# Seven block products instead of eight in the up projections of two feed-forward networks, with weight pools by tile size

## The chip, the cores and the metric

The kernel runs on one core of one Trainium2 chip. Its engines are TensorE (PE in the profile: matmuls; PEld: the loads of its stationary side), VectorE (DVE), ScalarE (ACT), GpSimd (POOL) and SyncE (SP), which here only starts transfers. The metric is the device time of one execution in microseconds (us), lower is better.

## The reference

Two blocks of a network on 512 tokens of width 1024 in f32. The first block has a feed-forward network (ffn1), a mixer, a cross attention and a second feed-forward network (ffn2); the second has a mixer, a plain network and an embedding branch. Only the two feed-forward networks are changed:

```python
D_MODEL, SEQ, D_FF = 1024, 512, 2816

def swiglu(x, w1, w3, w2):
    return (jax.nn.silu(x @ w1) * (x @ w3)) @ w2
...
        f = swiglu(rms_norm(h, ffn1_pre_g[l]), ffn1_w1[l], ffn1_w3[l], ffn1_w2[l])
        h = h + 0.5 * rms_norm(f, ffn1_post_g[l])
...
        f = swiglu(rms_norm(h, ffn2_pre_g[l]), ffn2_w1[l], ffn2_w3[l], ffn2_w2[l])
        h = h + 0.5 * rms_norm(f, ffn2_post_g[l])
```

## The kernel before

Everything is kept with features on the 128 partitions and the 512 tokens along the row: the width 1024 is 8 tiles, the hidden width 2816 is 22. A product has f32 accuracy by splitting both sides into a high part, rounded to the matmul's format, and the residue (low part), and doing three matmuls into the same bank: high by high, high by low, low by high (`mm3`, L283 to L285). So one output tile of an up projection is 8 x 3 = 24 matmuls of 512 columns.

A weight tile is loaded by SP into a raw buffer (`wr`), cast to its high part by ScalarE (`wh`, L246), and VectorE subtracts to get the residue (`wl`, L247). The pools hold 2 raw tiles and 5 of each part, each sized for 8 blocks of 128 x 128. In names of the profile x tiles are the normalised inputs, b, u and t tiles are slots of 512 elements, h the running state, `mm` and `lg` the banks of results.

`ffn` goes over the hidden tiles in chunks (6, 8 and 8 in ffn1; 7, 7 and 8 in ffn2). For a chunk it runs w1 and w3 for each tile, takes the product of the two with the activation (factors of the norm on VectorE, L560 and L564; activation on ScalarE; product on GpSimd, L565; split by ScalarE, L356, and VectorE, L357), and then projects the chunk down: 8 output tiles, each summed over the chunk's tiles and added to the sum so far (L543). The first 4 or 5 products of a stage run by halves of 256 tokens while the norm still computes (`begin`, with weights split into b and u slots: lead tiles). The last 5 or 4 outputs of the last down projection run by halves too: all first halves (A), then the second ones (B), which fill the time in which the next norm needs only A ("late" in the tables; kept in `self.rest`, run in `begin` of the next stage).

Each engine takes its instructions in the order that the program's scheduler wrote, and every engine waits for the others by semaphores; the order within one engine is fixed once the program is built.

Of the kernel before, what the change touches and what calls it, by code (L numbers as in the profile page):

```python
# [19 lines left out]
P = 128  # L20
# [147 lines left out]
BANKS = {k: v for k, v in K["banks"].items() if v}  # L168
SLOTS = dict(zip("btu", K["slots"]))


# [4 lines left out]
class Net:  # L176
    def __init__(self, ctx, tc, a):
        self.tc, self.nc, self.a = tc, tc.nc, a
        pool = lambda name, bufs, **k: ctx.enter_context(tc.tile_pool(name=name, bufs=bufs, **k))
        self.cp = pool("cp", 1)  # L180
        self.xp = pool("xp", 16)
        self.slots = {t: pool(t + "p", n) for t, n in SLOTS.items()}
        self.sp = pool("sp", 2)
        self.wr = pool("wr", 2)
        self.wh = pool("wh", 5)
        self.wl = pool("wl", 5)

# [12 lines left out]

        self.lead = self.nc.vector
# [30 lines left out]
    def pa(self):  # L232
        return self.bank("tt")


    def load(self, src, shape):

        nc = self.nc
        n = int(np.prod(shape[1:]))
        raw, hi, lo = (  # L240
            pool.tile([P, n], dt, tag=tag, name=self.nm(tag), padded_shape=[P, 8 * P])
            for pool, dt, tag in ((self.wr, F32, "wr"), (self.wh, F32R, "wh"), (self.wl, F32R, "wl")))
# [16 lines left out]
    def lead_weights(self, w, n, nk, k0=0, tag="b"):  # L259

        nc = self.nc
        raw = self.wr.tile([P, nk, P], F32, tag="wr", name=self.nm("wr"), padded_shape=[P, 8, P])
        src = self.a[w][n, :, k0 : k0 + nk, :]
# [16 lines left out]

    def mm3(self, ps, a, b, first, last):
        mm = self.nc.tensor.matmul
        mm(ps, lhsT=a[0], rhs=b[0], start=first, stop=False)  # L283
        mm(ps, lhsT=a[0], rhs=b[1], start=False, stop=False)  # L284
        mm(ps, lhsT=a[1], rhs=b[0], start=False, stop=last)  # L285

# [51 lines left out]
    def stream(self, jobs, tail=0, spare=0):  # L338
# [8 lines left out]
        for (_, _, xs, _, put), wt in zip(jobs[mid:], wts):  # L347
            put(self.lin(wt, xs, A), A)
            self.rest.append(lambda xs=xs, put=put, wt=wt: put(self.lin(wt, xs, B), B))

    def split(self, src, parts, scale=None):
# [198 lines left out]
    def ffn(self, pre, post, w1, w3, w2):  # L550
# [5 lines left out]
        def up(n):  # L556
# [11 lines left out]
            return u, [(w1, n, xs, 0, first), (w3, n, xs, 0, second)]  # L568

        c = 0  # L570
        for size in K["sizes:" + self.phase]:
            us, jobs = [], []
            for n in range(c, c + size):
# [848 lines left out]
```

## Time and profile before

| | us |
|---|---|
| Time, median of 3 runs | 2154.33 (2153.68 to 2159.0) |
| The profiled execution: its own time | 2151.55 |
| its span, first to last instruction | 2149.4 |
| TensorE busy in the span | 2083.3 (97%) |
| VectorE busy | 1287.4 (60%) |
| ScalarE busy | 907.5 (42%) |
| GpSimd busy | 309.2 (14%) |

Mean granted TensorE clock 0.989 of full. The program's stages lie one behind the other: ffn1's products from about 28 us to 385, ffn2's from about 945 to 1313. A busy share is a mean over the whole span; how much a saved microsecond of an engine is worth is told by the stretch in which it lies.

### The profile page before, as it was taken

The numbers are of one execution on the slowest core, as the hardware profiler recorded it, in microseconds if no ns is written. First come the engines' busy times: TensorE is split into PE (matmuls) and PEld (weight loads), VectorE is DVE, ScalarE is ACT, GpSimd is POOL, SyncE is SP. The second block draws the span as 40 slices with busy tenths as digits, with TensorE's granted clock in tenths as the row PEclk, the third lists the DMA queues.
The fourth block names the chain that finished last, engine by engine and source line by source line (L and its number), as shares of the span: only waits on it lengthen the run. The fifth ranks groups of instructions, "written<-read, shape, count | busy, mean of one in ns | idle before, by whom it ended". The sixth has DMA issues, their size and how long they took to land.

```text
span 2149.4 us, 27792 instructions
## 1 busy us (share of the span) xinstructions
PE 2083.3 (97%) x10718; PEld 1741.7 (81%) x10718; DVE 1287.4 (60%) x2427; ACT 907.5 (42%) x1603; POOL 309.2 (14%) x275
## 2 busy tenths in 40 slices
PE   8999999899999989999999998998999999999997
PEld 7788888878778888998787888876777888888887
DVE  6345344799875675574343447578987654444565
ACT  5222223673573453552222324467874422222352
POOL 2101011313431310041010113122100000000011
PEclk9999999999999999999999999998999999999999
DMA  5233333213223233322333232211013323333331
GB/s 161 86 107 89 97 92 110 69 48 101 89 70 98 79 112 104 99 78 72 97 92 103 89 112 71 74 50 44 28 47 89 118 69 89 97 94 93 108 99 40
DMA packets 60228, 186.15 MB, mean 87 GB/s; under 512 B 6336, under 2 KB 13504, under 8 KB 60096
## 3 DMA queue, kind: packets, MB, share of 16 engines
q1 hardware_dynamic: 57616, 180.97, 27.7%
q10 hardware_dynamic: 2448, 3.41, 0.5%
q8 instruction: 84, 1.38, 0.3%
q14 instruction: 48, 0.39, 0.1%
q0 software_dynamic: 32, 0.00, 0.0%
HBM read 182.25 MB, written 2.10 MB: 86 GB/s over the span
## 4 chain that ended last, share of the span: by engine, by line
PE 78%; DVE 11%; issue 4%; ACT 3%; DMA 2%; POOL 2%; SPq 0%; POOLq 0%; ACTq 0%; DVEq 0%
PE mm L284 13%; PE mm L283 13%; PE mm L285 13%; PE lg L283 11%; PE lg L284 11%; PE lg L285 11%; DVE wl L247 2%; DVE h L476 2%; PE tt L669 1%; DVE b L804 1%; DVE m L803 1%; PE o L684 1%; PE o L683 1%; ACT wh L246 1%; PE tt L428 1%
## 5 line engine op out<-in xcount | busy, mean ns | idle before, releaser
L246 ACT CAST wh<-wr 128x1024 fp32r<-128x1024 f32 (+3 forms) x314 | 325.7, 1038 | 756.4 <-PE lg L284 344.5
L247 DVE TENSOR_TENSOR wl<-wr,wh 128x1024 fp32r<-128x1024 f32 (+2 forms) x312 | 414.1, 1328 | 149.9 <-ACT wh L246 147.6
L283 PE MATMUL mm<-x,wh 128*128 128x512 f32 (+1 forms) x1080 | 416.7, 386 | 0.0
L284 PE MATMUL mm<-x,wh 128*128 128x512 f32 (+1 forms) x1080 | 415.7, 385 | 0.0
L285 PE MATMUL mm<-x,wl 128*128 128x512 f32 (+1 forms) x1080 | 415.3, 385 | 0.0
L283 PEld LDWEIGHTS mm<-x,wh 128*128 128x128 f32 x1080 | 203.3, 188 | 43.3 <-DVE v L1085 0.7
L285 PEld LDWEIGHTS mm<-x,wl 128*128 128x128 f32 x1080 | 203.2, 188 | 43.3
L284 PEld LDWEIGHTS mm<-x,wh 128*128 128x128 f32 x1080 | 203.3, 188 | 42.2
L283 PE MATMUL lg<-x,wh 128*128 128x512 f32 (+1 forms) x624 | 232.8, 373 | 0.0
L285 PE MATMUL lg<-x,wl 128*128 128x512 f32 (+1 forms) x624 | 232.7, 373 | 0.0
L284 PE MATMUL lg<-x,wh 128*128 128x512 f32 (+1 forms) x624 | 232.6, 373 | 0.0
L283 PE MATMUL mm<-b,wh 128*128 128x512 f32 (+1 forms) x493 | 175.5, 356 | 0.0
L284 PE MATMUL mm<-b,wh 128*128 128x512 f32 (+1 forms) x493 | 174.7, 354 | 0.4 <-DVE b L357 0.2
L285 PE MATMUL mm<-b,wl 128*128 128x512 f32 (+1 forms) x493 | 174.4, 354 | 0.0
L283 PE MATMUL lg<-b,wh 128*128 128x512 f32 (+1 forms) x455 | 161.4, 355 | 0.0
L284 PE MATMUL lg<-b,wh 128*128 128x512 f32 (+1 forms) x455 | 161.0, 354 | 0.0
L285 PE MATMUL lg<-b,wl 128*128 128x512 f32 (+1 forms) x455 | 161.0, 354 | 0.0
L565 POOL TENSOR_TENSOR t<-t,t 128x512 f32<-128x512 f32 (+1 forms) x48 | 66.4, 1383 | 578.2 <-ACT wh L246 486.7
L283 PEld LDWEIGHTS lg<-x,wh 128*128 128x128 f32 x624 | 117.4, 188 | 22.9
L285 PEld LDWEIGHTS lg<-x,wl 128*128 128x128 f32 x624 | 117.3, 188 | 22.9
L284 PEld LDWEIGHTS lg<-x,wh 128*128 128x128 f32 x624 | 117.3, 188 | 22.8
L356 ACT CAST b<-t 128x512 fp32r<-128x512 f32 (+1 forms) x100 | 58.7, 587 | 141.7 <-POOL t L565 67.9
(297 smaller groups left out, 3591.7 us busy)
## 6 DMA issues: line engine op xcount, KB each, us to landing
wr<-in_ffn_w SPq DMA_DIRECT2D x110, 512.0 KB, 3.6
wr<-in_w_in SPq DMA_DIRECT2D x64, 512.0 KB, 3.6
wr<-in_w_up SPq DMA_DIRECT2D x32, 512.0 KB, 3.6
wr<-in_w_down SPq DMA_DIRECT2D x32, 512.0 KB, 3.9
wr<-in_ffn_w SPq DMA_DIRECT2D x16, 448.0 KB, 3.4
wr<-in_w_out SPq DMA_DIRECT2D x8, 512.0 KB, 3.5
wr<-in_xattn_w_k SPq DMA_DIRECT2D x8, 512.0 KB, 3.5
wr<-in_xattn_w_v SPq DMA_DIRECT2D x8, 512.0 KB, 3.8
```

What stands on the lines that cost most here:

```text
L246: nc.scalar.copy(hi, raw)
L247: self.second.tensor_tensor(lo, raw, hi.bitcast(F32), op=OP.subtract)
L283: mm(ps, lhsT=a[0], rhs=b[0], start=first, stop=False)
L284: mm(ps, lhsT=a[0], rhs=b[1], start=False, stop=False)
L285: mm(ps, lhsT=a[1], rhs=b[0], start=False, stop=last)
L356: nc.scalar.copy(hi, src)
L428: nc.tensor.matmul(ps[:, i : i + 1], lhsT=acc[:, i * P : (i + 1) * P], rhs=self.ones, start=j == 0, stop=j == len(accs) - 1)
L476: nc.vector.scalar_tensor_tensor(h[k][:, tok], f, self.g(due[1], k), h[k][:, tok], op0=OP.mult, op1=OP.add)
L565: nc.gpsimd.tensor_tensor(t3[:, tok], t3[:, tok], t1[:, tok], op=OP.mult)
L669: nc.tensor.transpose(ps[:, b * P : b * P + P], p[:, j * P : j * P + P], self.ident)
L683: mm(o, lhsT=vj, rhs=hi, start=j == 0, stop=False)
L684: mm(o, lhsT=vj, rhs=lo, start=False, stop=j == last)
```

## The change

In both feed-forward networks the first 4 hidden tiles are computed as before. The other 18 are taken in 9 pairs. For a pair, each of w1 and w3 is a matrix of 2 x 2 blocks (two hidden tiles by two halves of the width, each half 4 tiles), the input is 2 x 2 blocks (halves of the width by halves of the tokens), and the 2 x 2 blocks of the result come from seven block products, not eight. One block product is 4 x 3 matmuls of 256 columns. `forms` makes the seven input operands once in each stage and splits each into high part and residue; `blocks` makes the weight operands of a pair and splits them; `fast` runs the products and adds them up, some in the banks and some by VectorE (`up2`), with copies kept by ScalarE. The chunks are now of 4, 4, 4, 4, 4 and 2 tiles. The factors of the norm, before multiplied to each result, are in the operands already; the product with the activation is on VectorE.

The weight pools are now by size for all stages: raw tiles for 6, 4 and 2 blocks of 256 elements (2, 3 and 1 buffers), parts for 4 and 2 (8 and 2 buffers). A weight of 8 blocks of 128 has therefore 4 pairs of parts where it had 5, and 3 raw buffers where it had 2. `mm3` passes a flag for sums that are continued, and the scratch size of dynamic transfers is set to 2048.

```diff
- 'sizes:ffn1': [6, 8, 8],
- 'sizes:ffn2': [7, 7, 8],
+ 'sizes:ffn1': [4, 4, 4, 4, 4, 2],
+ 'sizes:ffn2': [4, 4, 4, 4, 4, 2],
+ 'plain': 4,
...
+WEIGHTS = {"r6": 2, "r4": 3, "r2": 1, "w4": 8, "w2": 2}
...
-        self.wr = pool("wr", 2)
-        self.wh = pool("wh", 5)
-        self.wl = pool("wl", 5)
+
+        self.wp = {t: pool(t, n) for t, n in WEIGHTS.items()}
...
+    def weight(self, tag, n):
+        dt = F32 if tag[0] == "r" else F32R
+        return self.wp[tag].tile([P, n], dt, tag=tag, name=self.nm(tag[0]), padded_shape=[P, 256 * int(tag[1])])
...
+    def forms(self, gain, r):
+
+        nc, h = self.nc, self.h
+        two = lambda alloc, dt: [alloc((P, S), dt).rearrange("p (k t) -> p k t", k=2) for _ in range(2)]
+        out = {}
+
+        def scaled(c, half, alloc=self.tmp):
+            t, tok = two(alloc, F32), HALVES[half]
+            for k in range(4):
+                nc.vector.scalar_tensor_tensor(
+                    t[k // 2][:, k % 2], h[4 * c + k][:, tok], self.g(gain, 4 * c + k), r[:, tok], op0=OP.mult, op1=OP.mult)
+            return t
+
+        def combined(x, y, op):
+            t = two(self.tmp, F32)
+            for o, i, j in zip(t, x, y):
+                nc.vector.tensor_tensor(o, i, j, op=op)
+            return t
+
+        def parts(name, src, alloc):
+            hi, lo = two(alloc, F32R), two(alloc, F32R)
+            for t, i, j in zip(src, hi, lo):
+                nc.scalar.copy(i, t)
+                nc.vector.tensor_tensor(j, t, i.bitcast(F32), op=OP.subtract)
+            out[name] = [(hi[k // 2][:, k % 2], lo[k // 2][:, k % 2]) for k in range(4)]
+
+
+        b11, b12 = scaled(0, 0), scaled(0, 1)
+        t1 = combined(b11, b12, OP.subtract)
+        parts("11", b11, self.big)
+        b21 = scaled(1, 0, lambda shape, dt: self.big(shape, dt))
+        parts("21", b21, self.big)
+        b22 = scaled(1, 1)
+        t2 = combined(b22, t1, OP.subtract)
+        parts("1", t1, self.big)
+        parts("2", t2, self.xt)
+        parts("22", b22, self.xt)
+        parts("3", combined(b22, b12, OP.add), self.xt)
+        parts("4", combined(b21, t2, OP.subtract), self.xt)
+        return out
+
+    def blocks(self, w, n):
...
+        one, two, three, four = tiles("r4", 2), tiles("r6", 3), tiles("r4", 2), tiles("r2", 1)
+
+        nc.sync.dma_start(one, src[n].rearrange("p (b k) c -> p b (k c)", b=2))
+        nc.sync.dma_start(two[:, 0:2], src[n + 1].rearrange("p (b k) c -> p b (k c)", b=2))
+        nc.vector.tensor_tensor(two[:, 2], two[:, 0], one[:, 0], op=OP.subtract)
+        nc.vector.tensor_tensor(three, two[:, 1:2].to_broadcast([P, 2, c]), two[:, 0::2], op=OP.subtract)
+        nc.vector.tensor_tensor(four[:, 0], one[:, 1], three[:, 1], op=OP.subtract)
+        out = []
+        for tag, raw in (("w4", one), ("w4", three), ("w2", four), ("w4", two[:, 1:3])):
+            m = raw.shape[1]
+            hi, lo = tiles(tag, m), tiles(tag, m)
+            nc.scalar.copy(hi, raw)
+            nc.vector.tensor_tensor(lo, raw, hi.bitcast(F32), op=OP.subtract)
+            out += [[(hi[:, b, k * P : k * P + P], lo[:, b, k * P : k * P + P]) for k in range(4)] for b in range(m)]
+        return dict(zip(("11", "12", "1", "2", "4", "22", "3"), out))
+
+    def fast(self, jobs, b):
...
+        for w, n, put in jobs:
+            a = self.blocks(w, n)
+            x = self.bank("lg")[:, : S // 2]
+            product(x, a["11"], b["11"], True, True)
+            p1 = kept(x)
+            z = self.bank("mm")[:, : S // 2]
+            product(z, a["12"], b["21"], True, True)
+            put(0, A, z, p1)
+            y = self.bank("mm")[:, : S // 2]
+            product(y, a["1"], b["1"], True, True)
+            p5 = kept(y)
+            product(x, a["2"], b["2"], False, True)
+            u = kept(x)
+            for go in late:
+                go()
+            product(y, a["4"], b["22"], False, True)
+            put(0, B, y, u)
+            product(x, a["3"], b["3"], False, True)
+            put(1, B, x, p5)
+
+            def last(x=x, a=a, put=put):
+                product(x, a["22"], b["4"], False, True)
+                put(1, A, x, None)
+
+            late = [last]
+        for go in late:
+            go()
...
+            def first(i, tok, ps, t):
+                if t is not None:
+                    nc.vector.tensor_tensor(t1[i][:, tok], t, ps, op=OP.add)
...
+                nc.scalar.activation(t1[i][:, at], ps if t is None else src[:, at], AF.Silu)
+
+            def second(i, tok, ps, t):
+                if t is None:
+                    nc.vector.tensor_tensor(t3[i][:, tok], t1[i][:, tok], ps, op=OP.mult)
+                else:
+                    nc.vector.tensor_tensor(t3[i][:, tok], t, ps, op=OP.add)
...
+                    nc.vector.tensor_tensor(t3[i][:, at], t3[i][:, at], t1[i][:, at], op=OP.mult)
+                if i == 0 or t is None:
+                    self.split(t3[i], u[i])
...
-            self.stream(jobs)
+                self.stream(jobs)
+                b = self.forms(pre, r)
+            for n in range(c + plain, c + size, 2):
+                u, j = up2(n)
+                us += u
+                quick += j
+            self.fast(quick, b)
             self.down(w2, f, c, us, c > 0, K["late:" + self.phase] if c + size == KF else (0, 0))
```

What moves on VectorE, first place: the end of the first chunk of ffn1, where the last hidden tile of the chunk is put together and the weights of the first projection down follow. Before, L564 is the last result, L357 its residue, and the L247 of 768 elements are residues of down weights:

```order
L564 TENSOR_TENSOR t_164<-lg_810,rows_134 128x512
L247 TENSOR_TENSOR wl_945<-wr_943,wh_944 128x768
L357 TENSOR_TENSOR b_166<-t_164,b_165 128x512
L247 TENSOR_TENSOR wl_971<-wr_969,wh_970 128x768
L247 TENSOR_TENSOR wl_997<-wr_995,wh_996 128x768
L247 TENSOR_TENSOR wl_1023<-wr_1021,wh_1022 128x768
L247 TENSOR_TENSOR wl_1081<-wr_1079,wh_1080 128x1024
```

After, the last result is L680, L473 is its residue, L250 of 512 elements are residues of down weights (the first row below is that of the third output), and L368, L375 and L382 are the scaled half tiles, combinations and residues of `forms`; left out are 32 more rows of these and the L473:

```order
L250 TENSOR_TENSOR w_839<-r_837,w_838 128x512
L680 TENSOR_TENSOR t_162<-lg_672,rows_140 128x512
L368 SCALAR_TENSOR_TENSOR t_701<-h_100,gains,rows_140 128x256
L368 SCALAR_TENSOR_TENSOR t_701<-h_101,gains,rows_140 128x256
...
L375 TENSOR_TENSOR t_786<-b_726,t_746 128x512
L382 TENSOR_TENSOR x_780<-t_774,x_778 128x512
L250 TENSOR_TENSOR w_859<-r_857,w_858 128x512
L382 TENSOR_TENSOR x_791<-t_785,x_789 128x512
L250 TENSOR_TENSOR w_879<-r_877,w_878 128x512
L382 TENSOR_TENSOR x_792<-t_786,x_790 128x512
L250 TENSOR_TENSOR w_899<-r_897,w_898 128x512
```

The residues of the fourth and later down weights have moved behind the forms; before, they followed the last result at once. ScalarE's casts stand in the same way: 13 of the forms' 14 casts ahead of the high part of the fifth down weight.

Second place: VectorE in the middle of a chunk's products. Before, for each product one result (L560 or L564) and one residue of 1024 elements (L247), and for each hidden tile one residue of the split (L357):

```order
L564 TENSOR_TENSOR t_1048<-lg_1118,rows_134 128x512
L247 TENSOR_TENSOR wl_1285<-wr_1283,wh_1284 128x1024
L357 TENSOR_TENSOR b_1050<-t_1048,b_1049 128x512
L560 TENSOR_TENSOR t_1051<-mm_1153,rows_134 128x512
L247 TENSOR_TENSOR wl_1318<-wr_1316,wh_1317 128x1024
L564 TENSOR_TENSOR t_1052<-lg_1186,rows_134 128x512
L247 TENSOR_TENSOR wl_1353<-wr_1351,wh_1352 128x1024
L357 TENSOR_TENSOR b_1054<-t_1052,b_1053 128x512
L560 TENSOR_TENSOR t_1055<-mm_1221,rows_134 128x512
```

After, a stretch of one product of w3 in ffn1 (L412 to L414 combine raw weights, L420 their residues, L693 add for w1, L703 and L707 add and multiply for w3, L473 the split's residues; sh are ScalarE's kept copies):

```order
L420 TENSOR_TENSOR w_1220<-r_1210,w_1219 128x1024
L413 TENSOR_TENSOR r_1338<-r_1337 128x1024
L420 TENSOR_TENSOR w_1224<-r_1212,w_1223 128x1024
L420 TENSOR_TENSOR w_1232<-r_1211,w_1231 128x1024
L703 TENSOR_TENSOR t_963<-sh_1165,mm_1138 128x256
L420 TENSOR_TENSOR w_1228<-r_1213,w_1227 128x512
L707 TENSOR_TENSOR t_963<-t_963,t_961 128x512
L703 TENSOR_TENSOR t_964<-sh_1151,lg_1109 128x256
L414 TENSOR_TENSOR r_1339<-r_1336,r_1338 128x512
L473 TENSOR_TENSOR b_958<-t_963,b_957 128x512
L707 TENSOR_TENSOR t_964<-t_964,t_962 128x256
L693 TENSOR_TENSOR t_969<-sh_1248,mm_1250 128x256
```

The residues and combinations that stand between the results belong to later products: r_1210 to r_1213 are the raw weights of the next one (w1 of the next pair), r_1336 to r_1338 those of the one behind it.

## Rows read from the trace of the kernel before

**Rows 1.** The page, part 1: busy us (share of the span) and instructions by engine.

```profile
PE 2083.3 (97%) x10718; PEld 1741.7 (81%) x10718; DVE 1287.4 (60%) x2427; ACT 907.5 (42%) x1603; POOL 309.2 (14%) x275
```

**Rows 2.** The page, part 4: the chain that ended last, by engine.

```profile
PE 78%; DVE 11%; issue 4%; ACT 3%; DMA 2%; POOL 2%; SPq 0%; POOLq 0%; ACTq 0%; DVEq 0%
```

**Rows 3.** Windows: stretch, length, busy us of PE, PEld, DVE, ACT, POOL, clock, DMA.

```profile
46.00:372.00 326.00, 325.74 (x1462) 264.79 (x1461) 139.69 (x140) 91.70 (x119) 31.92 (x24) 1.00 0.32 98
372.00:474.00 102.00, 91.35 (x568) 81.44 (x567) 86.19 (x194) 70.22 (x154) 29.38 (x35) 0.95 0.18 52
957.00:1303.00 346.00, 345.56 (x1586) 282.69 (x1586) 146.53 (x160) 96.96 (x130) 37.21 (x26) 1.00 0.32 96
1303.00:1368.00 65.00, 58.95 (x434) 55.62 (x433) 51.34 (x135) 28.75 (x61) 16.79 (x19) 0.97 0.20 61
```

**Rows 4.** Timeline of PE in ffn1 (start, duration in us, instruction), 512 columns.

```profile
100.27 0.40 PE L283 MATMUL mm<-b,wh 128*128 128x512 f32 x1
...
103.77 0.39 PE L283 MATMUL lg<-b,wh 128*128 128x512 f32 x1
```

**Rows 5.** Timeline of PE, matmuls of 256 columns: lead tiles, then the end of ffn1.

```profile
31.43 0.28 PE L283 MATMUL mm<-x,b 128*128 128x256 f32 x1
...
35.98 0.28 PE L285 MATMUL lg<-x,b 128*128 128x256 f32 x1
...
370.78 0.28 PE L283 MATMUL mm<-b,wh 128*128 128x256 f32 x1
...
382.82 0.28 PE L283 MATMUL mm<-b,wh 128*128 128x256 f32 x1
...
385.42 0.28 PE L285 MATMUL mm<-b,wl 128*128 128x256 f32 x1
```

**Rows 6.** Timeline of DVE, queued instructions of four sizes.

```profile
386.79 0.41 DVE L475 TENSOR_TENSOR b<-b,rows 128x256 f32<-128x256 f32 x1
387.13 0.68 DVE L277 TENSOR_TENSOR b<-wr,b 128x512 fp32r<-128x512 f32 x1
387.73 0.41 DVE L415 TENSOR_TENSOR sh<-sh,sh 128x256 f32<-128x256 f32 x1
...
388.67 0.47 DVE L360 SCALAR_TENSOR_TENSOR x<-h,gains,x 128x256 fp32r<-128x256 f32 x1
389.06 0.68 DVE L277 TENSOR_TENSOR b<-wr,b 128x512 fp32r<-128x512 f32 x1
...
2026.13 1.22 DVE L247 TENSOR_TENSOR wl<-wr,wh 128x1024 fp32r<-128x1024 f32 x1
2027.27 0.69 DVE L357 TENSOR_TENSOR b<-t,b 128x512 fp32r<-128x512 f32 x1
```

**Rows 7.** Groups of instructions by line, 46 to 372 us, shapes apart.

```profile
L247 DVE TENSOR_TENSOR wl<-wr,wh 128x1024 fp32r<-128x1024 f32 x50 | 78.8, 1576 | 24.4 <-ACT wh L246 24.4
...
L246 ACT CAST wh<-wr 128x1024 fp32r<-128x1024 f32 x50 | 52.7, 1054 | 174.1 <-PE lg L284 90.9 <-PE mm L284 70.7 <-issue 8.2
...
L565 POOL TENSOR_TENSOR t<-t,t 128x512 f32<-128x512 f32 x20 | 28.5, 1427 | 275.5 <-ACT wh L246 226.4 <-DVE t L564 49.1
```

**Rows 8.** Timeline of PE behind ffn1, then windows (columns of rows 3).

```profile
389.19 0.38 PE L284 MATMUL lg<-x,u 128*128 128x256 f32 x1 [1.77 <-DVE x L360]
...
409.91 0.35 PE L283 MATMUL mm<-x,u 128*128 128x256 f32 x1 [2.12 <-DVE t L598]
...
390.00:395.00 5.00, 3.87 (x20) 3.67 (x21) 5.00 (x13) 2.86 (x7) 0.00 (x0) 0.74 0.63 197
410.00:415.00 5.00, 3.50 (x17) 2.89 (x17) 5.00 (x9) 4.32 (x11) 3.13 (x4) 0.79 0.01 2
```

**Rows 9.** Timeline of DVE, then of ACT, behind the last first half of ffn1.

```profile
370.98 0.42 DVE L543 TENSOR_TENSOR b<-b,lg 128x256 f32<-128x256 f32 x1 [0.79 <-PE lg L285]
...
377.55 0.37 ACT L444 COPY rows<-tt 128x256 f32<-128x256 f32 x1 [2.45 <-PE tt L439]
...
380.50 0.50 ACT L359 ACTIVATE x<-h,gains 128x256 fp32r<-128x256 f32 x1
```

More of the change, by code (lines that the diff above doesn't have):

```diff
@@ L239, in load @@
         n = int(np.prod(shape[1:]))
-        raw, hi, lo = (
-            pool.tile([P, n], dt, tag=tag, name=self.nm(tag), padded_shape=[P, 8 * P])
-            for pool, dt, tag in ((self.wr, F32, "wr"), (self.wh, F32R, "wh"), (self.wl, F32R, "wl")))
+        raw, hi, lo = (self.weight(tag, n) for tag in ("r4", "w4", "w4"))
         names = " ".join(f"d{i}" for i in range(len(shape) - 1))
@@ L261, in lead_weights @@
         nc = self.nc
-        raw = self.wr.tile([P, nk, P], F32, tag="wr", name=self.nm("wr"), padded_shape=[P, 8, P])
+        raw = self.weight("r4", nk * P).rearrange("p (k c) -> p k c", c=P)
         src = self.a[w][n, :, k0 : k0 + nk, :]
@@ L279, in lead_weights, with mm3, mm @@
         return out
[L281 to L285, printed above, removed]
+    def mm3(self, ps, a, b, first, last, on=False):
+        def mm(lhsT, rhs, start, stop):
+            self.nc.tensor.matmul(ps, lhsT=lhsT, rhs=rhs, start=start, stop=stop, skip_group_check=on)
+        mm(a[0], b[0], first, False)
+        mm(a[0], b[1], False, False)
+        mm(a[1], b[0], False, last)
     def lin(self, wt, xs, tok=ALL, bank=None):
@@ new lines, in blocks, with tiles @@
+    def blocks(self, w, n):
+        nc, src = self.nc, self.a[w]
+        c = 4 * P
+        def tiles(tag, m):
+            return self.weight(tag, m * c).rearrange("p (b c) -> p b c", c=c)
+        one, two, three, four = tiles("r4", 2), tiles("r6", 3), tiles("r4", 2), tiles("r2", 1)
[12 more added lines that the diff above has]
+        return dict(zip(("11", "12", "1", "2", "4", "22", "3"), out))
@@ new lines, in fast, with product, kept @@
+    def fast(self, jobs, b):
+        late = []
+        def product(ps, a, x, first, last):
+            for k in range(4):
+                self.mm3(ps, a[k], x[k], first and k == 0, last and k == 3, True)
+        def kept(ps):
+            t = self.sp.tile([P, S // 2], F32, tag="sh", name=self.nm("sh"), bufs=K["sqb"])
+            self.nc.scalar.copy(t, ps)
+            return t
+        for w, n, put in jobs:
[23 more added lines that the diff above has]
+            go()
@@ L568, in up, with up2 @@
             return u, [(w1, n, xs, 0, first), (w3, n, xs, 0, second)]
+        def up2(n):
+            t1, t3, u = ([self.tmp(), self.tmp()] for _ in range(2)), None, [self.pair(), self.pair()]
+            t1, t3 = t1
+            def first(i, tok, ps, t):
+                if t is not None:
+                    nc.vector.tensor_tensor(t1[i][:, tok], t, ps, op=OP.add)
+                if i == 0 and tok == A:
+                    return
+                src, at = (t1[i], ALL) if i == 0 else (t1[i], tok)
+                nc.scalar.activation(t1[i][:, at], ps if t is None else src[:, at], AF.Silu)
[4 more added lines that the diff above has]
+                    nc.vector.tensor_tensor(t3[i][:, tok], t, ps, op=OP.add)
+                    if i == 0 and tok == A:
+                        return
+                    at = ALL if i == 0 else tok
+                    nc.vector.tensor_tensor(t3[i][:, at], t3[i][:, at], t1[i][:, at], op=OP.mult)
+                if i == 0 or t is None:
+                    self.split(t3[i], u[i])
+            return u, [(w1, n, first), (w3, n, second)]
         c = 0
+        b = None
         for size in K["sizes:" + self.phase]:
-            us, jobs = [], []
-            for n in range(c, c + size):
+            us, jobs, quick = [], [], []
+            plain = K["plain"] if c == 0 else 0
+            for n in range(c, c + plain):
                 u, j = up(n)
```

2 lines of the change are left out of this document (1 added, 1 removed).

## The prediction

> **What bounds the kernel now.** I read the page's busy shares first: the tensor engine is busy for 2083.3 of 2149.4 us, VectorE for 1287.4, ScalarE for 907.5, GpSimd for 309.2 [rows 1]. The chain that ended last agrees: 78% matmul, 11% VectorE [rows 2]. Then the windows of the two stages that change: ffn1 has the tensor engine busy for 325.74 of 326 us and ffn2 for 345.56 of 346, with VectorE at 140 and 147 and ScalarE at 92 and 97 [rows 3]. So in both feed-forward stages every microsecond of matmul taken out is worth a microsecond, until VectorE, which does the new additions, is full. In the stages behind them (372 to 474 and 1303 to 1368) the tensor engine waits already [rows 3], so what is hidden in a stage's last matmuls can come back there as a wait.
>
> **Matmuls saved.** In 18 of the 22 hidden tiles of each ffn, a pair of tiles by one weight matrix took 2 x 8 x 3 = 48 matmuls of 512 columns and takes 7 x 4 x 3 = 84 of 256. There are 9 pairs, 2 matrices and 2 stages: 36 such products. A 512-column matmul starts every (103.77 - 100.27) / 15 = 0.2333 us [rows 4]: 11.20 us a product. The 256-column step decides everything else, and the trace has three. With the stationary side in the small lead tiles it is (35.98 - 31.43) / 38 = 0.1197 us; in the half passes that end ffn1, with weights from the weight pool, it is (385.42 - 382.82) / 23 = 0.1130 us in an undisturbed piece, and (385.42 - 370.78) / 125 = 0.1171 us over the whole stretch, which holds six small matmuls of the norm [rows 5]. The new products take their weights from the pool, as the half passes do, so I take 0.115: 84 x 0.115 = 9.66 us, a gain of 1.54 us a product and **55 us** in all. The bounds are 0.1130 (61 us) and 0.1197 (41 us). It breaks even at 11.20 / 84 = 0.1333.
>
> The Trainium skill (TensorE: Matmul & The Clock Gate, section "Wait — 56ns, not 53.3ns?") gives columns divided by 2.4 GHz plus 2.5 ns for a warm matmul, an estimate of 0.2158 and 0.1092 us here. By it the gain would be 36 x (48 x 0.2158 - 84 x 0.1092) = 43 us: the shorter matmul would carry relatively more of the fixed part. The rows show the opposite, with weights from the pool a 512-column step is more than twice the 256-column one in the undisturbed piece, so the measurement decides.
>
> **Additions in the new products.** For each of the 36, VectorE does two 512-element combinations, one of 1024, three residues of 1024 and one of 512: by steps of queued work, 1024 elements take 2027.27 - 2026.13 = 1.14 us, 512 take 387.73 - 387.13 = 0.60, 256 take 387.13 - 386.79 = 0.34 and a scaled 256 take 389.06 - 388.67 = 0.39 [rows 6]. That is 4 x 1.14 + 3 x 0.60 = 6.36 us. The results add 1.0 us for w1 (three of 256) and 3.5 us for w3 (five of 256 and three of 512). A pair costs 2 x 6.36 + 4.5 = 17.2 us of VectorE against 2 x 9.66 = 19.3 us of matmul: 89%. ScalarE has per pair six casts of 1024 (1.05 [rows 7]), two of 512, six kept copies of 256 and the activations, about 12.5 us, and is no bound. GpSimd's product (1.43 us [rows 7]) drops out there. Durations of VectorE beside GpSimd are longer (1.58 for 1024 on average over ffn1 [rows 7]); by them a pair would cost over 20 us. Since GpSimd has nothing in these stretches I take the steps. In the order of the changed program the residues of the next product stand about half a product (5 us) ahead of their use, so the tensor engine should seldom wait; but results and residues share one in-order queue. I allow 0.15 us a product, **5 us**, with bounds 0 and 25.
>
> **Six chunks instead of three.** Each boundary must turn the last hidden tile into two parts before the projection down can finish its first output; the late product and the first down matmuls lie over that. Three more boundaries in each stage at about 0.4 us: **+2.4 us** (0 to 6). The accumulation on VectorE grows from 16 to 40 additions of 512 a stage (0.60 each, 14 us), hidden under the matmuls of the down stretches (22.4 us for a four-tile chunk, VectorE about 20).
>
> **The forms, once in each stage.** This is the largest cost. They come between the four plain tiles and their projection down: 16 scaled half tiles, 10 combinations and 14 residues on VectorE, 16 x 0.39 + 24 x 0.60 = 20.6 us, and 14 casts on ScalarE. The order shows the residue of the fourth down weight behind all forms but two residues on VectorE's queue, and the hi cast of the fifth behind 13 of the 14 casts on ScalarE's. From the end of the last plain product (T) VectorE reaches that residue at T + 0.6 + 0.6 + 19.4 + 0.6 = T + 21.2. The tensor engine has three outputs ready: 3 x 12 x 0.2333 = 8.4 us, with about 1 us lost before the first (the last tile's chain of VectorE, GpSimd 1.43 [rows 7], ScalarE and VectorE is some 3.5 us long, and only three of the four tiles, 2.1 us, cover it). It then waits from about T + 9.4 to T + 21.2: 12 us. After waits of 2 us and less the granted clock fell to 0.74 and 0.79 of full in windows of 5 us (behind a wait of 2.12 us in the second) [rows 8]: 5 x (1 - 0.74) = 1.3 us lost, more with the window behind it; after a longer one I take 1.7 at the 1.2 GHz level. Per stage 12 + 1 + 1.7 - 0.7 for what the pause lets VectorE catch up = 14 us, **+28 us** for both. Bounds: 20, two bare waits of 10 us, if VectorE slips some residues of the down weights in earlier and the clock costs nothing, and 36 at the single durations of VectorE (0.47 and 0.68 [rows 6]), by which the forms take 24 us.
>
> **The stage's end.** ffn1's end now leaves five half passes of 24 matmuls behind the last first-half output at 370.78; the tensor engine works on them until 385.42 [rows 5], and under them the norm runs: the last sum at 370.98, the row of factors at 377.55, the first normalised tile at 380.50 [rows 9]. The last chunk has two tiles afterwards: each half pass is six matmuls, partly done before, and some 1.9 us of cover are left for a chain of 9.5 us. A wait of about 7 us appears before the first matmul of the next stage. Most of it comes back, since the half passes that were the cover have been done by then and the wait of 1.77 us at 389.19 and 2.12 at 409.91 [rows 8] should shrink. I count 3 us a stage, **+6 us** (0 to 15).
>
> **Weight pools.** Eight-block weights have four pairs of buffers instead of five, so where five half passes are kept, one must run before the last first half. That matters at the ends of the mixer and of the cross attention: **+1 us** (-3 to +5). A third raw buffer loads earlier. Queues: SP issues the same bytes in the same order. The DMA scratch size costs nothing: its queues are not what the chain waits for [rows 2].
>
> **Sum**, on the profiled execution of 2151.55 us (span 2149.4), which is 2.8 us below the median of the timed runs, 2154.33: -55 + 5 + 2.4 + 28 + 6 + 1 = -13, so 2139 in the profile, and about **2141 us** as a median.
>
> **Rivals.**
> - *The forms' wait is smaller than the queue says*, because the tensor engine finds other work or VectorE is quicker: 20 instead of 28, and the pool's step of 0.113 (61 instead of 55): 2141 - 8 - 6 = 2127. For it: 0.113 is what the undisturbed pieces show. 0.2.
> - *VectorE becomes the bound in the new products.* At 0.5 us or more of waiting per product it takes over: 36 x 0.7 = 25 instead of 5 gives 2161, slower than before. For it: 89% load in an in-order queue in which a result waiting for its matmul holds back the residues behind it, and the longer durations of [rows 7]. Against: those durations come with GpSimd busy beside. The point from which it decides is a mean wait of 0.52 us a product. 0.15.
> - *The 256-column step is 0.1197*: 14 us of gain less, 2155, no change. Against: that step is found with lead tiles only [rows 5]. 0.1. The rule of the Trainium skill above (TensorE: Matmul & The Clock Gate) would lead to nearly the same time, an estimate of 2153.
> - *Waits add up at the stage ends* with 15 us instead of 6 and pools at 5: 2154. 0.07.
>
> The forecast itself (2131 to 2149) has 0.48. A measurement here tells apart about 0.3%, 6.5 us, so faster is below 2147.9. Part of the forecast's own range touches that, which leaves faster 0.67, same 0.17, slower 0.16. Eight in ten lie between 2119 and 2159, which takes in the smaller wait and the 0.1197 step, and leaves out most of the VectorE bound.
>
> **What would show it.** In the changed profile: 256-column steps of 0.113 to 0.117 in the up stretches; a wait of the tensor engine of 11 to 13 us once in each ffn behind the third output of the first down stretch, released by the residue of a down weight; VectorE at 85 to 92% of the new stretches; waits of 5 to 8 us at the ends of the two stages. It is wrong if many short waits on residues stand in the new products (VectorE is the bound), if the step is near 0.12, or if the one long wait is not there.

## The result, and the profile after

The changed kernel takes 2172.14 us (median of 4 runs, 2170.52 to 2173.57), the kernel before 2155.98 on the same occasions: the ratio is 1.0074, 95% interval 1.0056 to 1.0091, so it is slower by 0.7% where 2141 was forecast. The profiled execution took 2171.57 us with a span of 2169.8 and a mean granted clock of 0.971; the one of before (2151.55 us) was below all of its timed runs, so spans differ by 20.4 us where medians differ by 16.2. The sums below go by the spans.

The busy shares and the chain by engine of the changed kernel, which answer to [rows 1] and [rows 2]:

```profile
PE 2056.6 (95%) x11852; PEld 1774.4 (82%) x11852; DVE 1488.0 (69%) x2869; ACT 1031.5 (48%) x1877; POOL 252.0 (12%) x239
...
PE 85%; DVE 8%; ACT 3%; issue 2%; POOL 2%; DMA 0%; SPq 0%; ACTq 0%; POOLq 0%; DVEq 0%
```

TensorE is busy for 26.7 us less than before and the program is 20.4 us longer: 47 us of waiting are new. The new products alone took out some 55 us of matmul (worked out below), so the rest of the matmuls is busy for some 29 us longer than before; the lower granted clock, 0.971 against 0.989, is one cause of that, and it was not taken apart further. The windows of the changed kernel say where not to look and where to look. Columns as in [rows 3]; the first is the products of one four-tile chunk, the second its projection down, the third the end of ffn1, the fourth the first leads of ffn2:

```profile
95.53:134.73 39.20, 39.20 (x340) 38.71 (x339) 28.50 (x42) 21.78 (x37) 0.00 (x0) 1.00 0.37 113
134.73:156.57 21.84, 21.84 (x96) 17.25 (x95) 17.11 (x24) 7.30 (x10) 0.00 (x0) 1.00 0.31 96
372.00:390.00 18.00, 8.78 (x47) 8.14 (x45) 16.47 (x45) 10.89 (x26) 7.74 (x10) 0.66 0.50 168
940.00:950.00 10.00, 6.18 (x28) 5.19 (x27) 9.38 (x16) 8.18 (x20) 3.93 (x5) 0.71 0.41 117
```

In the chunk TensorE never waits. At the end of ffn1 it is busy for 8.78 of 18 us, at a mean granted clock of 0.66 (before, the same 18 us had half passes in them until 385.42 [rows 5]), and ffn2's leads begin at 6.18 of 10 us busy and 0.71.

The clearest reading is by landmarks. The leads of a stage (its first products, on halves of the tokens) end with a matmul that is easy to find in each trace; the distances between these ends are the stages. The table has the distances in us of the traces named below (ffn1's column runs from its own leads' end to the mixer's, "mixer, cross" from there to ffn2's, "ffn2" to the second mixer's, "mixer 2" to the plain network's; what follows is the same in all):

```
                                     ffn1   mixer, cross   ffn2   mixer 2
before                              393.6          538.2  384.3     382.8
after                               392.8          557.6  382.4     387.0
pools alone (e1_pairs4_only)        399.4          558.2  387.6     387.5
short last chunk alone (e9)         410.5          537.9  398.9     383.5
after, forms in pieces (e4)         377.8          552.5  375.4     387.2
after, 5 pairs (e5)                 392.5          541.7  386.3     384.9
after, plain products (e8)          411.2          554.5  406.5     386.2
forms in pieces, 5 pairs (e6)       382.0          539.6  379.6     385.0
the same, 4 tiles last (e7)         384.0          540.4  371.9     384.2
forms in pieces, chunks of 6 (e10)  380.9          556.0  364.0     388.1
```

From before to after the two changed stages gain only 0.8 and 1.9 us, and the two stages in which no product was changed lose 19.4 and 4.2. Between kernels with the same four pairs and 4-tile chunks the column "mixer, cross" differs by 5 us (552.5 to 557.6) though no code differs there, so a few us in one cell are no finding by themselves.

The forms' wait is where it was expected. PE in the first projection down of ffn1, the idle time before an instruction and its releaser in brackets:

```profile
68.50 0.62 PE L287 MATMUL lg<-b,w 128*128 128x512 f32 x2
79.28 0.80 PE L287 MATMUL mm<-b,w 128*128 128x512 f32 x1 [10.15 <-ACT w L249]
80.52 0.80 PE L287 MATMUL lg<-b,w 128*128 128x512 f32 x1 [0.44 <-DVE w L250]
```

Three outputs are done; the two matmuls at 68.50 are the first of the fourth. The next one in the queue belongs to the fifth output and starts at 79.28, when ScalarE's cast of the fifth down weight is there: 10.15 us of waiting. Then 0.44 more go by until VectorE's residue of the fourth weight, which stands behind the forms, as the order said:

```profile
79.79 0.67 DVE L250 TENSOR_TENSOR w<-r,w 128x512 fp32r<-128x512 f32 x1
```

The same pair of waits stands at 1024 us in ffn2.

PE at the end of ffn1, behind its last half pass:

```profile
378.44 0.66 PE L555 MATMUL tt<-ident,r 128*128 128x128 f32 x2 [4.61 <-DVE r L505]
...
385.05 0.58 PE L287 MATMUL lg<-x,u 128*128 128x256 f32 x1 [4.45 <-ACT x L475]
```

4.61 us for the norm's factor, 4.45 for the first normalised tile. Before, there was no wait at this place: the first lead matmul of the mixer followed the last half pass [rows 5] at once.

```profile
385.54 0.28 PE L283 MATMUL lg<-x,u 128*128 128x256 f32 x1
```

It starts at 385.05 now: by the end of ffn1 nearly all that the products had brought was gone. At the end of ffn2 the same two waits are 3.97 us (at 1322.25) and 2.77 us (at 1327.17).

### The profile page after: what moved, and what is told of

Same layout as the page of the kernel before. It is cut to its first block, busy times and chain, and to the rows that moved or that the text cites. A ratio compares the mean times of both kernels' runs of the same rounds, so it can differ in the third digit from the quotient of the medians.

```text
span 2169.8 us, 30997 instructions
## 1 busy us (share of the span) xinstructions
PE 2056.6 (95%) x11852; PEld 1774.4 (82%) x11852; DVE 1488.0 (69%) x2869; ACT 1031.5 (48%) x1877; POOL 252.0 (12%) x239
## 3 DMA queue, kind: packets, MB, share of 16 engines
q1 hardware_dynamic: 64528, 180.97, 26.5%
## 4 chain that ended last, share of the span: by engine, by line
PE 85%; DVE 8%; ACT 3%; issue 2%; POOL 2%; DMA 0%; SPq 0%; ACTq 0%; POOLq 0%; DVEq 0%
PE mm L287 44%; PE lg L287 34%; DVE h L592 1%; PE tt L820 1%; PE tt L544 1%; PE o L834 1%; PE o L835 1%; POOL b L890 1%; PE lg L785 1%; PE lg L786 1%; DVE t L368 1%; DVE b L591 1%; DVE w L250 0%; DVE x L476 0%; ACT w L249 0%
## 5 line engine op out<-in xcount | busy, mean ns | idle before, releaser
L287 PE MATMUL mm<-x,w 128*128 128x512 f32 (+1 forms) x2808 | 606.4, 366 | 0.5 <-DVE w L250 0.5
L287 PEld LDWEIGHTS mm<-x,w 128*128 128x128 f32 x2808 | 476.2, 189 | 90.2 <-DVE w L250 1.0
L249 ACT CAST w<-r 128x1024 fp32r<-128x1024 f32 (+2 forms) x290 | 258.8, 893 | 486.5 <-PE mm L287 221.7
L287 PE MATMUL mm<-b,w 128*128 128x512 f32 (+1 forms) x2253 | 413.7, 334 | 23.2 <-ACT w L249 20.3
L287 PEld LDWEIGHTS mm<-b,w 128*128 128x128 f32 x2253 | 337.9, 190 | 74.0 <-ACT w L249 21.5
L250 DVE TENSOR_TENSOR w<-r,w 128x1024 fp32r<-128x1024 f32 (+2 forms) x288 | 297.6, 1034 | 113.6 <-ACT w L249 106.0
L287 PE MATMUL lg<-x,w 128*128 128x256 f32 (+1 forms) x2304 | 365.7, 312 | 0.0
L287 PE MATMUL lg<-b,w 128*128 128x512 f32 (+1 forms) x1725 | 342.3, 349 | 6.6 <-DVE w L250 6.4
L287 PEld LDWEIGHTS lg<-x,w 128*128 128x128 f32 x2304 | 319.8, 188 | 33.1 <-DVE t L703 2.0
L287 PEld LDWEIGHTS lg<-b,w 128*128 128x128 f32 x1725 | 279.4, 192 | 53.2 <-DVE w L250 7.8
L420 DVE TENSOR_TENSOR w<-r,w 128x1024 fp32r<-128x1024 f32 (+1 forms) x144 | 155.5, 1087 | 22.7 <-ACT w L419 21.1
L473 DVE TENSOR_TENSOR b<-t,b 128x512 fp32r<-128x512 f32 (+1 forms) x100 | 64.2, 642 | 14.8 <-ACT b L472 14.3
```

The costliest lines, as they stand in the source:

```text
L287: self.nc.tensor.matmul(ps, lhsT=lhsT, rhs=rhs, start=start, stop=stop, skip_group_check=on)
L420: nc.vector.tensor_tensor(lo, raw, hi.bitcast(F32), op=OP.subtract)
L473: nc.vector.tensor_tensor(lo, src, hi.bitcast(F32), op=OP.subtract)
```

## The experiments

All are compared with the kernel before on the same chip; its medians there were 2154.9 to 2156.1 us.

**e1_pairs4_only**: the kernel before with one part of the change, the pools for its weights of 8 blocks: 4 pairs of parts instead of 5, and 3 raw buffers instead of 2.

```diff
-        self.wr = pool("wr", 2)
-        self.wh = pool("wh", 5)
-        self.wl = pool("wl", 5)
+        self.wr = pool("wr", 3)
+        self.wh = pool("wh", 4)
+        self.wl = pool("wl", 4)
```

> The kernel before with one thing of the change alone: 4 pairs of weight parts and 3 raw buffers instead of 5 pairs and 2; no block products, chunks as before. Theory (the missing fifth pair holds back the last first half at the ends of stages, and the changed kernel loses some 20 us between the last matmuls of ffn1 and the leads of the later stages): 2155 + 20 = about 2175 us, with the end of the cross attention's leads some 8 to 16 us later. Rival (the pairs cost nothing, the loss behind the stages comes from the short last chunk and the slower clock behind its waits): 2155 us, within 4.

Measured: 2188.03 us, ratio 1.0152 (1.0137 to 1.0167). The pools alone cost 33 us, 13 more than the theory and more than the whole change: 20.0 between the leads of the mixer and of ffn2 (19.4 in the changed kernel), 4.7 in the second mixer (4.2), 5.8 and 3.3 in the two feed-forward stages. How it comes about is seen at the end of the cross attention, where eight half passes are kept: the weights of three are split into x tiles, those of the other five take pairs from the pool. In the trace of before, the last matmul of the attention, ACT's cast of the fifth of these weights, PE's turning of the first half's factors into a row, and the first lead matmul of ffn2 start at:

```profile
889.63 0.39 PE L285 MATMUL o<-u,b 128*128 128x512 f32 x1
...
892.62 1.05 ACT L246 CAST wh<-wr 128x1024 fp32r<-128x1024 f32 x1 [1.63 <-DMA wr<-in_xattn_w_o]
...
914.29 0.38 PE L439 MATMUL tt<-ident,r 128*128 128x128 f32 x2
...
933.65 0.36 PE L283 MATMUL lg<-x,u 128*128 128x256 f32 x1
```

In the changed kernel the last matmul of the attention starts at 896.38 (the row has the last two), and the other three are:

```profile
896.16 0.62 PE L287 MATMUL o<-u,b 128*128 128x512 f32 x2
...
921.14 1.05 ACT L249 CAST w<-r 128x1024 fp32r<-128x1024 f32 x1 [2.34 <-PE lg L287]
...
932.71 0.40 PE L555 MATMUL tt<-ident,r 128*128 128x128 f32 x2 [0.99 <-DVE r L505]
...
940.22 0.28 PE L287 MATMUL lg<-x,u 128*128 128x256 f32 x1
```

The cast waited for a PE matmul, the second half of an output whose weights held the pair. The first half of the last output, and with it the norm, came 18.4 us later (932.71 against 914.29), and second halves that should have covered the norm had been used up before. Of the 18.4 us the program had lost 6.8 before this place (896.38 against 889.63), and 11.7 come here. In e1, the same cast, with the same wait and the same releaser, on ACT:

```profile
929.18 1.05 ACT L246 CAST wh<-wr 128x1024 fp32r<-128x1024 f32 x1 [2.34 <-PE lg L284]
```

In e1 about half of the 20 us is lost here too: this row of factors comes 26.5 us later than before (940.76 against 914.29), the row of factors ahead of it 15.2 us (815.89 against 800.70). The other half goes bit by bit between the mixer's leads and there and was not taken apart. In this run the third raw buffer came together with the loss of a pair; that the pair is what costs rests on the row above, in which the cast waits for a matmul and not for its transfer.

**e2_late4**: the changed kernel with a half pass less at three ends.

```diff
- 'late:ffn1': [5, 0],
+ 'late:ffn1': [4, 0],
...
- 'late:mix': [5, 0],
+ 'late:mix': [4, 0],
...
- 'late:cross': [8, 3],
+ 'late:cross': [7, 3],
```

> The changed kernel with one half pass fewer at the ends of ffn1, the mixer and the cross attention (4, 4 and 7 instead of 5, 5 and 8), so that the weights of the half passes fit the 4 pairs. Theory (the fifth half pass waits for a pair, and with it the next norm): the norm starts some 5 us earlier at two stage ends, 2172 - 10 = about 2162 us. Rival (the half passes' cover is what is short, whatever the pairs): 2.7 us less cover at each of three ends, 2172 + 3 to 8 us.

Measured: 2170.03 us, ratio 1.0066 (1.0051 to 1.0082): 2 us, between the two expectations. At the end of the cross attention, ACT, then PE:

```profile
903.87 1.05 ACT L249 CAST w<-r 128x1024 fp32r<-128x1024 f32 x1 [3.61 <-PE lg L287]
...
927.23 0.40 PE L555 MATMUL tt<-ident,r 128*128 128x128 f32 x2
...
945.82 0.35 PE L544 MATMUL tt<-ones,sf 128*128 128x1 f32 x2 [4.00 <-DVE sf L533]
```

The last cast came at 903.87 instead of 921.14 and the factor's row at 927.23 instead of 932.71, though this program's attention ended 2.9 us later (899.24 against 896.38) and one output more ran at full width first. So the list that fits lets the norm start earlier. But the half passes then ended before the second half's sum was there (4.00 us of waiting at 945.82). The stage from the mixer's leads to ffn2's gained 4 us by it (553.6 instead of 557.6), and ffn1 and ffn2 lost 2 each. With four pairs, giving up a half pass is about as dear as letting it wait.

**e3_last4**: the changed kernel with the short chunk second.

```diff
- 'sizes:ffn1': [4, 4, 4, 4, 4, 2],
- 'sizes:ffn2': [4, 4, 4, 4, 4, 2],
+ 'sizes:ffn1': [4, 2, 4, 4, 4, 4],
+ 'sizes:ffn2': [4, 2, 4, 4, 4, 4],
```

> The changed kernel with the chunk of 2 tiles moved from the end to the second place, so the last chunk has 4 tiles and each half pass at the stage's end 12 matmuls instead of 6. Theory (the wait of about 10 us at the end of each feed-forward stage is missing cover): 5 and 4 half passes get 0.7 us more each, before and behind the last first half, so 3 to 6 us less at each of two ends: about 2163 us. Rival (the chain of the norm or the pairs of weights set that end): 2172 within 3.

Measured: 2168.99 us, ratio 1.0069 (1.0052 to 1.0086): 3 us less than the changed kernel, which does not tell the two apart by itself. By the landmarks its two feed-forward stages are 2.1 and 1.8 us shorter, less than the 3 to 6 of the theory; four pairs may hold back the longer half passes of ffn1, which was not tried apart. e9 takes the cover alone, and e7 makes this move with five pairs.

**e4_spread**: the forms in pieces. `forms` became a generator with a yield after each operand, the operands that need no x tile first; the pieces go between the remaining plain products and between the outputs of the first projection down.

```diff
-                self.stream(jobs)
-                b = self.forms(pre, r)
+                pieces = self.forms(pre, r)
+                for job in jobs:
+                    self.stream([job])
+                    b = next(pieces)
+                for _ in range(4 - len(jobs)):
+                    b = next(pieces)
...
+        for job in jobs:
+            self.stream([job])
+            next(between, None)
```

> The changed kernel with the same forms issued in pieces: three quarters of the first half between the last plain products, the rest between the outputs of the first projection down. Theory (the two waits of 10.5 us with the slower clock behind them come only from where the forms stand in VectorE's queue): both waits nearly vanish, 2172 - 25 = about 2147 us. Rival (VectorE has no room there, the wait moves to the plain products or to the first block product): 2172 - 5 or less gained.

Measured: 2147.17 us, ratio 0.9961 (0.9947 to 0.9976), 25 us less than the changed kernel, as the theory had it. PE in the same stretch as above:

```profile
62.10 0.50 PE L287 MATMUL mm<-b,w 128*128 128x512 f32 x1 [0.87 <-ACT b L479]
...
72.91 2.60 PE L287 MATMUL mm<-b,w 128*128 128x512 f32 x10 [0.70 <-DVE w L250]
```

The wait of 10.15 us is gone, two of 0.87 and 0.70 us are left, with the same instructions of VectorE. In ffn2 three of 2.2, 0.8 and 0.7 us on down weights are left. By the table ffn1 and ffn2 gain 15.0 and 7.0 us, 22 in all; another 5.1 lie in mixer and cross, which this edit does not touch (the spans of the two traces differ by 26.8).

**e5_five_pairs**: the changed kernel with 5 pairs. They fit because the small parts of a block product come from free b slots and one raw buffer is given up.

```diff
-WEIGHTS = {"r6": 2, "r4": 3, "r2": 1, "w4": 8, "w2": 2}
+WEIGHTS = {"r6": 2, "r4": 2, "r2": 1, "w4": 10}
...
-            hi, lo = tiles(tag, m), tiles(tag, m)
+            part = tiles if tag == "w4" else lambda *_: self.big((P, S)).rearrange("p (b c) -> p b c", c=c)
+            hi, lo = part(tag, m), part(tag, m)
```

> The changed kernel with 5 pairs of weight parts again: the two small parts of a block product come from the free b slots, and there are 2 raw buffers of the 4-block size instead of 3. Theory (the missing pair costs the changed kernel some 20 us between the mixer's leads and the plain network): 2172 - 20 = about 2152 us, with the leads of ffn2 ending 12 us or more earlier against the leads of the mixer. Rival (the stage ends are long because the last chunk is short; pairs matter only to long half passes): 2172 - 6 or less gained, or lost to the missing raw buffer.

Measured: 2157.57 us, ratio 1.0002 (0.999 to 1.0013): 14.6 us less than the changed kernel, somewhat short of 20. Mixer and cross take 541.7 us instead of 557.6, the second mixer 384.9 instead of 387.0: 18 us come back in these two stages. At the end of the cross attention the cast waits for its transfer only and the factor's row is where it was in the kernel before (ACT, then PE):

```profile
891.41 1.05 ACT L249 CAST w<-r 128x1024 fp32r<-128x1024 f32 x1 [1.03 <-DMA r<-in_xattn_w_o]
...
914.14 0.38 PE L556 MATMUL tt<-ident,r 128*128 128x128 f32 x2
```

Some of it is given away in the block products, four of which now take 40.1 to 40.2 us instead of 39.20 (columns of [rows 3]):

```profile
95.29:135.50 40.21, 40.21 (x340) 39.91 (x339) 32.30 (x47) 22.37 (x39) 0.00 (x0) 1.00 0.43 130
219.71:259.80 40.09, 40.09 (x341) 39.69 (x339) 29.13 (x44) 20.69 (x36) 0.00 (x0) 1.00 0.35 105
```

That is 0.9 us for four of 36 products, some 8 us in all. What two raw buffers do there, or the b slots, was not taken apart.

**e6_spread_five**: both edits.

> The changed kernel with both: forms in pieces, and 5 pairs. Theory (two separate causes that add): 2147 - 20 = about 2127 us, 28 us faster than before. Rival (with 2 raw buffers and more of VectorE's work in the first chunk the two get in each other's way): 2140 or more.

Measured: 2139.01 us, ratio 0.9921 (0.99 to 0.9942). The two gains do not add in full: 8 us less than e4, where e5 had gained 14.6, so the rival's 2140 is nearer than the theory's 2127. By the table, mixer and cross gain 12.9 over e4, and each feed-forward stage loses 4.2.

**e7_spread_five_last4**: both edits and the short chunk second.

> As the kernel with both, and the chunk of 2 tiles second instead of last. With 5 pairs the longer half passes at the end of the feed-forward stages are usable: theory (cover at the stage's end counts): 4 to 8 us less than the kernel with both. Rival (the end is set by the chain of the norm alone): the same within 3 us.

Measured: 2131.65 us, ratio 0.9899 (0.9864 to 0.9934): 7.4 us less than e6, 24 less than the kernel before and the best of all (three of its four runs lie at 2130.8 to 2131.9, one at 2140.8). The gain is in ffn2 (371.9 instead of 379.6); ffn1 is 2 us longer, with the chunk behind the short one slower by some 5 us: 44.67 us for its products where the others take 40.09, with two waits of 1.6 and 0.7 us for its first weights in it.

**e8_plain_chunks**: the changed kernel without block products and forms, in its chunks and with its pools.

```diff
-            plain = K["plain"] if c == 0 else 0
+            plain = size
...
-                self.stream(jobs)
-                b = self.forms(pre, r)
+            self.stream(jobs)
```

> The changed kernel without its block products and forms: all 22 hidden tiles as before, but in the chunks 4, 4, 4, 4, 4, 2 and with the changed pools. Against the changed kernel it tells what products and forms bring together; against the kernel before with 4 pairs (2188) what the chunks cost. Theory (36 products bring 50 us, forms take 28, the short last chunk takes about 8 in each stage): 2172 + 22 = about 2194 us, and 2188 + 8 or so. Rival (the products bring little, and the pools take everything): 2172 within 5, below the 2188 of the pools alone.

Measured: 2212.36 us, ratio 1.0262 (1.0243 to 1.0282). It is 18 us more than the theory and 40 us slower than the changed kernel, so block products and forms together do bring time, and 24 slower than e1, which has the same pairs and longer chunks. With the forms' 25 us the products are worth 65 in it. Some of that is a wait at each chunk's end that the plain form has and the block products have not: at 62.88, 131.45, 200.01, ... the next matmul starts 1.47 us later instead of 0.23. PE's waits from 40 to 380 us (total, times, longest):

```profile
PE mm L287 <- ACT b L472: 5.5, 5, 1.2
```

With a sixth at the end of ffn1 and as many in ffn2, the later starts make some 14 us.

**e9_short_last**: the kernel before with the last chunk cut in two.

```diff
- 'sizes:ffn1': [6, 8, 8],
- 'sizes:ffn2': [7, 7, 8],
+ 'sizes:ffn1': [6, 8, 6, 2],
+ 'sizes:ffn2': [7, 7, 6, 2],
```

> The kernel before, pools and products as they were, with the last chunk cut in two: 6, 8, 6, 2 and 7, 7, 6, 2 instead of 6, 8, 8 and 7, 7, 8. Theory (the short last chunk by itself opens the wait at the end of both feed-forward stages, since its half passes have 6 matmuls instead of 24): 8 to 10 us in each stage and 1.2 us for one more boundary, 2155 + 20 = about 2175 us. Rival (with 5 pairs and GpSimd's help the norm's chain is covered anyway; the wait comes from the pools and from VectorE's new work): 2155 + 5 or less.

Measured: 2186.61 us, ratio 1.0146 (1.0131 to 1.0161). 31.6 us for a short last chunk alone, with 5 pairs and none of the new work: 16.9 in ffn1, 14.6 in ffn2, nothing elsewhere. PE at the end of its ffn1, then a window over that place:

```profile
392.97 0.66 PE L439 MATMUL tt<-ident,r 128*128 128x128 f32 x2 [3.82 <-DVE r L389]
...
401.26 0.58 PE L283 MATMUL lg<-x,u 128*128 128x256 f32 x1 [6.13 <-ACT x L359]
```

```profile
385.00:402.00 17.00, 6.98 (x46) 6.62 (x46) 14.31 (x43) 9.55 (x24) 7.82 (x9) 0.73 0.35 107
```

The waits for the same two things as in the changed kernel, 3.82 and 6.13 us, and a mean granted clock of 0.73 around them.

**e10_spread_six**: forms in pieces and chunks 4, 6, 6, 6.

```diff
- 'sizes:ffn1': [4, 4, 4, 4, 4, 2],
- 'sizes:ffn2': [4, 4, 4, 4, 4, 2],
+ 'sizes:ffn1': [4, 6, 6, 6],
+ 'sizes:ffn2': [4, 6, 6, 6],
```

> The changed kernel with the forms in pieces and the chunks 4, 6, 6, 6: the same block products, two boundaries less in each stage, and a last chunk of 6 tiles, with the changed pools (4 pairs). Theory (cover at the stage's end): the half passes have 18 matmuls instead of 6, 6 to 10 us less in each stage than the kernel with the forms in pieces, 2147 - 14 = about 2133 us. Rival (with 4 pairs the fifth half pass is blocked, longer passes block it longer): 2147 or more.

Measured: 2140.94 us, ratio 0.9931 (0.9915 to 0.9948): 6.2 us less than e4, between the two expectations. ffn2 gains 11.4 us, ffn1 loses 3.1 and the mixer with the cross attention 3.5. PE's longest wait behind ffn1 there:

```profile
PE mm L287 <- DVE t L766: 7.2, 1, 7.2
```

ffn1 keeps five half passes with 4 pairs, ffn2 keeps four, which fit. That the fifth is the difference is argued from e1 and e2; it was not tried in this kernel.

## Why the prediction was wrong

**The products: right.** A chunk's products and projection down take 39.20 + 21.84 = 61.04 us; 96 down matmuls at 0.2333 [rows 4] are 22.4, which leaves 38.6 us for four products, 9.66 each. That is the forecast's number, with no wait of TensorE in the chunk, so the 55 us are there and the 5 us allowed for VectorE's queue were not spent. (0.115 was a choice between two rows; that it fits to the last digit is luck.) The rival of VectorE as the bound is refuted: it is busy for 28.50 + 17.11 = 45.6 of 61.04 us, 75%. The sign of 85 to 92% was not met: it is 73% in the products, since part of their work runs under the projection down (78%). The groups of VectorE in that chunk's 61 us (columns as in [rows 7]) show the small durations, without GpSimd beside:

```profile
L420 DVE TENSOR_TENSOR w<-r,w 128x1024 fp32r<-128x1024 f32 x13 | 15.8, 1220 | 2.1 <-ACT w L419 2.1
...
L413 DVE TENSOR_TENSOR r<-r 128x1024 f32<-128x1024 f32 x4 | 4.9, 1220 | 0.1
...
L412 DVE TENSOR_TENSOR r<-r,r 128x512 f32<-128x512 f32 x4 | 2.8, 690 | 3.8 <-DMA r<-in_ffn_w 3.8
...
L414 DVE TENSOR_TENSOR r<-r,r 128x512 f32<-128x512 f32 x4 | 2.7, 682 | 0.0
```

The residues of 1024 elements take 1.22 us, not the mean of 1.58 of [rows 7]. That mean was of two kinds: of the 50 in the kernel before, 31 ran with GpSimd idle and took 1.23 us, and of the 19 that met GpSimd's product 15 took 2.31 to 2.34. The 256-column step was the pool's, so the rival at 0.1197 is out as well.

The fixed part per matmul in the Trainium skill (TensorE: Matmul & The Clock Gate, section "Wait — 56ns, not 53.3ns?") would have given a lower gain, an estimate of 43 us. The chunk gives 55, and the measurement decides.

**The forms: right.** +28 us were forecast, a wait of 12 us once in each stage; measured are waits of 10.15 and 0.44 us, and by e4 25 us, or 22 in the two stages alone. The residue of the fourth down weight, forecast for 21.2 us behind the last plain product, ended at 80.46, 21.3 us behind the end of that product at 59.13. That is closer than the sum deserved: `forms` has 8 combinations and not 10, which takes 1.2 us from it, and its first four scaled tiles took about a microsecond longer than their steps. For the 1.7 us of slower clock no row stood behind the number; over 80 to 90 us the granted clock was 0.79, some 2.1 us.

**The stage's end: the step that was mis-sized first.** The forecast saw the wait (about 7 us before the next stage's first matmul) and then took most of it back: "I count 3 us a stage". Nothing came back: the term of +6 us stands against some 27. That is by difference: the spans differ by 20.4 us, of which -55.4 are the products, 25 the forms and 23.6 the pools, which leaves 27, some 13 a stage, or 30 with e4's 22. This holds what the pools cost at these ends (5.8 and 3.3 us in e1). e8, with the same chunks and pools, comes to the same: its two stages are 39.8 us longer than before, 14 of that waits at chunk ends, which leaves 25. And e9 shows 31.6 for a last chunk of two tiles in the kernel before, where the waits at chunk ends took at most 1.3 us a stage. The wait itself is 4.61 + 4.45 = 9.1 us at ffn1 and 3.97 + 2.77 = 6.7 at ffn2, near the 7 of the forecast. But behind it the first matmuls of the next stage ran at the lower clock level (a granted clock of 0.66 over 372 to 390, 0.50 over 380 to 390), and the waits that should have shrunk did not: the one of 2.12 us at 409.91 [rows 8] is one of 2.47 us at 410.47 now. The half passes were not work that could be done at any time. They were the work at that place that needs nothing of the norm.

**The weight pools: the step that failed outright.** "+1 us (-3 to +5)" stands against 19.4 + 4.2 = 23.6 in the two stages in which nothing else was changed (15.9 + 2.1 = 18.0 of which came back with five pairs in e5), and 33 alone in e1. The forecast named the mechanism (a fifth half pass must wait for a pair) and priced it as one reordered pass. It left out what is late next: the held first half is the last of eight outputs, the norm needs the sum over all eight, and the second halves that must run to free the pair are those that were to cover that norm. So the norm starts later and its cover is gone at once.

The rival that named both steps (waits add up at the stage ends, with 15 us and pools at 5) had a chance of 0.07 and, at 2154, prices that were too low by far. The range's upper end of 2159 took in neither, and the signs of being wrong all looked at the products and the forms: none of them came, and the forecast was wrong all the same.

**Boundaries: next to nothing.** +2.4 was forecast; the four-tile chunks of block products follow each other without a wait, since the late product lies over the split, as forecast. Only the chunk of two tiles waits, 0.53 us at 359.42 and 0.5 in ffn2.

## What to carry to other kernels

Work that filled a wait was paid for twice here when the change took it: once as the wait itself, and once as the slower clock behind it. So, for each stage's end, list what TensorE can do between the last input of the norm and its first output, and count it anew after every change of chunk sizes.

A buffer count is part of the order. Compare the number of operands that the tail keeps alive with the number of buffers, and follow the instruction that would wait for the missing one to what depends on it, before counting the buffer as cheap.

One-off preparation belongs between the instructions that others wait for, not ahead of them: the same forms in pieces cost 25 us less here. With the pieces, five pairs and a longer last chunk the block products do pay (2131.65 us, 1.0% below the kernel before).

## What was not expected of the hardware

Two waits with little work between them cost more of the clock than one that was longer than both together. Windows of the changed kernel (columns of [rows 3]), behind the forms' wait of 10.15 us, which ends at 79.28, and behind the waits of 4.61 and 4.45 us at the end of ffn1, the last of which ends at 385.05, with some 2 us of matmuls between them:

```profile
79.28:84.28 5.00, 4.56 (x10) 3.27 (x11) 4.02 (x7) 1.75 (x3) 0.00 (x0) 0.52 0.39 114
84.28:89.28 5.00, 5.00 (x23) 4.01 (x23) 3.12 (x5) 2.64 (x4) 0.00 (x0) 1.00 0.59 201
...
385.05:390.05 5.00, 4.84 (x20) 4.42 (x20) 5.00 (x12) 3.08 (x7) 2.13 (x3) 0.50 0.58 197
390.05:395.05 5.00, 4.18 (x21) 4.02 (x21) 4.31 (x11) 2.49 (x7) 0.25 (x1) 0.53 0.00 0
```

Behind the one wait the clock was at the lower level (1.2 GHz) for about 5 us and then full; behind the two it stayed there for nearly 10. TensorE was busy almost throughout in the first case, and paused again for 0.82 us at 391.03 in the second; which of the differences kept the clock down was not tried.
